# Later low parts, a later sample burst and later transpositions in the openings of two FFNs

## The chip, the cores and the metric

The kernel runs on one core of a Trainium2 chip. The metric is the device time of one launch in microseconds (us). The kernel before takes 2395.5 us, the median of three runs (2390.06 to 2398.54). One further execution was profiled; it took 2394.01 us, and its span from the first to the last instruction is 2392.4 us.

## The reference, cut to what matters

One decoder layer is computed for a prompt of 1024 tokens and a sample of 8 sequences of 4 new tokens, with D = 1024 and an FFN width of 2816:

```
x = x + 0.5 * gate0 * swiglu(modulated(x, g_ffn1, 0), w1_gate, w1_up, w1_down)
x = x + gate1 * mixers(modulated(x, g_mix, 1))          # attention beside gated MLP
x = x + 0.5 * gate2 * swiglu(modulated(x, g_ffn2, 2), w2_gate, w2_up, w2_down)
swiglu(h) = (silu(h @ w_gate) * (h @ w_up)) @ w_down
modulated(h) = rms_norm(h) * (1 + scale) + shift
```

The change lies in the first few dozen microseconds of the two swiglu lines.

## The kernel before, in words

**Engines and order.** Each engine works through its own queue in the order in which the program issues to it; the order is written out by hand. TensorE (PE) does the matmuls, ScalarE (ACT) copies and activations, VectorE (DVE) and GpSimd (POOL) the additions and subtractions, SyncE (SP) issues the loads. Nearly all tiles of the 1 MB-and-less kind share one pool of 46 buffers (`NU = 46`), and a load into a buffer waits for the last user of the tile that was there.

**Numbers in two parts.** A matrix is kept as a high part (rounded, made on ACT) and a low part (what is left, made on DVE as source minus high part). A product is three matmuls of 512 columns, high by high, high by low, low by high: `mm3`, L324 to L326. For token tiles the high part is `x_hi` (L742), the low part `x_lo` (L746); `x_put` does one right after the other. For weights of a block it is `split` (L330, L331).

**The FFN.** The 2816 hidden columns are done in 11 blocks of 256. Blocks 1 to 10 use a Strassen form with seven products, whose operands are tokens (B11, B21, B22), differences of tokens (T1 to T4) and sums of weights (`sums_s`, L256 to L259, four POOL additions `wsum`). Block 0 is done in the plain way, and meanwhile the differences are made: that is the opening. It has four stages (half, kh) = (0,0), (0,1), (1,0), (1,1), each of 48 matmuls: tokens 0 to 3 first, then 4 to 7, and the lower and upper half of D in turn. After each two `mm3` (six matmuls) `tick(1.36)` is called, so a stage has eight ticks, called turns 1 to 8 below.

**Fillers.** What is not block 0's own work is written as generators. A filler has a step cost (`every`) and a start value; each tick adds 1.36 to its account, and for each `every` in the account it is moved on to its next `yield`. `finish()` runs a generator to its end at once. `mid1` and `mid2` say which generators run in which stage of the first and second FFN:

- (0,0) of the first FFN: `second()` (L1822): the statistics of tokens 4 to 7 (Square on ACT L525, power on POOL L518 and L519, scaling on DVE L531), then `rows` for B12: for each of four j's four transpositions on PE (L553), their eviction on ACT (L756), `x_hi`, and the low part one j behind.
- (0,1): `rows` for B22, then `T1()`; beside it the sample's norm `s_norm`, which ends with two transpositions (L610) and the copy `xsT` on DVE (L612).
- (1,0): `T23()`, and `s_ffn_gu` for block 0 of the sample: a burst of 32 matmuls (L622) of the sample's rows against the unconverted weights of block 0, a copy `G` on DVE (L644), and two yields later the fold (`s_fold`: four transpositions L628, a reduction on DVE L630, a Silu on ACT L649, a product on DVE L651).
- (1,1): `T4()`, the loads of block 1's first weights and, at its middle, their `sums_s`.

In `T1`, `T23` and `T4` each step makes one difference (L776; T1 and T2 on DVE, T3 and T4 on POOL), then the high part on ACT and the low part on DVE:

```
sub_(nc.vector, t, f1[j][:, 1], f0[j][:, 0])                   # T2
sub_(nc.gpsimd, f1[j][:, 0], f1[j][:, 1], f1[j][:, 0])         # T3
self.x_put(X, "T2", j, t)
yield
```

`fin` (L863, L865) turns block 0's sums in PSUM into hidden rows: on ACT for the gate, on DVE for the up product. Block 1 begins with the product A11, whose weights are split into two parts just then; its third matmul needs the low part that DVE makes (L331).

Of the kernel before, what the change touches and what calls it, by code (L numbers as in the profile page):

```python
# [87 lines left out]
class Step:  # L88
# [682 lines left out]
    def x_rest(self, X, xs, sub, f0):  # L771


        nc = self.nc
        f1, t2 = [], []
        sub_ = lambda eng, o, x, y: eng.tensor_tensor(out=o, in0=x, in1=y, op=ALU.subtract)  # L776

        def rows(i, name):
            last = None
            for j in range(4):  # L780
                if not i:
                    f1.append(self.u([P, 2, 512], F32, name="xf"))
                self.x_tr(xs, sub, j, i, f1[j])
                w = self.x_hi(f1[j][:, i])
                if last:
                    self.x_lo(X, name, *last)
                last = (j, f1[j][:, i], w)
                yield
            self.x_lo(X, name, *last)
            yield  # L790

        def T1():
            for j in range(4):
                t = f0[j][:, 0]
                sub_(nc.vector, t, f1[j][:, 0], t)
                self.x_put(X, "T1", j, t)
                yield

        def T23():
            for j in range(4):  # L800
                if j % 2 == 0:
                    t2.append(self.u([P, 2, 512], F32, name="xt"))
                t = t2[j // 2][:, j % 2]
                sub_(nc.vector, t, f1[j][:, 1], f0[j][:, 0])
                sub_(nc.gpsimd, f1[j][:, 0], f1[j][:, 1], f1[j][:, 0])
                self.x_put(X, "T2", j, t)
                yield
                self.x_put(X, "T3", j, f1[j][:, 0])
                yield

        def T4():
            for j in range(4):
                t = f0[j][:, 1]
                sub_(nc.gpsimd, t, t, t2[j // 2][:, j % 2])
                self.x_put(X, "T4", j, t)
                yield

        return rows(0, "B12"), rows(1, "B22"), T1(), T23(), T4()

    def prod(self, un, X, ps, start=True, js=range(4), la=2):  # L820
# [940 lines left out]
def build(tc, a, o, stop=None):  # L1761
    with ExitStack() as ctx, tc.manual_schedule():
        k = Step(tc, a, o, ctx, stop)
# [8 lines left out]
        plan1 = k.plan_ffn("w1")  # L1772
        plan_m = k.plan_in()
        plan_p = [k.plan_post(hf == 1) for hf in range(2)]
        plan2 = k.plan_ffn("w2")
# [44 lines left out]
        f1a, f1b, T1, T23, T4 = k.x_rest(X1, xsb1, 0, f01)  # L1820

        def second():  # L1822

            for t in range(4, 8):
                xsb1.append(k.norm_stats(t, 0))
            for t in range(4, 8):
                k.norm_scale(t, 0, xsb1[t - 4])
            yield
            yield from f1a

        def chain(*gs):
            for g in gs:
                yield from g

        def mid1(stage):
            if stage == (0, 0):
                k.f1 = k.add(second(), 1.6)
            elif stage == (0, 1):
                k.f1.finish()
                for q in (2, 3):  # L1840
                    k.ada_q(q, k.psb)
                for q in (2, 3):
                    k.ada_m(q)
                for q in (2, 3):
                    k.x_mod(X1, f01, q)
                k.f1 = k.add(chain(f1b, T1), 1.1)
                k.f2 = k.add(k.s_norm(0, k.ada_rows()), 0.95)
            elif stage == (1, 0):
                k.f1.finish()
                k.f2.finish()  # L1850
                k.f1 = k.add(T23, 1.2)
                k.f2 = k.add(k.s_ffn_gu(plan1["b"][0]), 1.2)
            elif stage == (1, 1):
                k.f1.finish()
                k.f2.finish()
                k.f1 = k.add(T4, 1.3)
            elif stage == (2, 0):
                k.f1.finish()
            elif stage == 3:
                k.ad = k.add(k.ada_gen([2, 3, 4, 5], 4, 8), 2.6, 12.0)  # L1860
                k.ad.step()
# [8 lines left out]
        def after1(t):  # L1870
# [6 lines left out]
            if t == 3:  # L1877
                k.need(3, 4)
                k.norm_scale(3, 1, xs1[3])
                k.f1 = k.add(k.norm_T(xs1[0:4], 1, nT[0], k.psa), 4.0)  # L1880

        acc = k.ffn(plan1, X1, lambda: k.need(2) or k.gate[0], load_xp, mid1, after1)
        k.f1.finish()
        k.norm_scale(7, 1, xs1[7])
# [29 lines left out]
        f1 = k.add(k.c_T(cn1, 1), 1.3, 2.6)  # L1914
# [118 lines left out]
        def mid2(stage):  # L2033
            if stage == (0, 0):
                k.f1 = k.add(f1a2, 1.1, 5.5)
            elif stage == (0, 1):
                k.f1.finish()
                k.f1 = k.add(chain(f1b2, T1_2), 1.1)
                k.f2 = k.add(k.s_norm(2), 1.4)
            elif stage == (1, 0):  # L2040
                k.f1.finish()
                k.f2.finish()
                k.f1 = k.add(T23_2, 1.2)
                k.f2 = k.add(k.s_ffn_gu(plan2["b"][0]), 1.2)
            elif stage == (1, 1):
                k.f1.finish()
                k.f2.finish()
                k.f1 = k.add(T4_2, 1.3)
            elif stage == (2, 0):
                k.f1.finish()  # L2050
            elif stage == 3:
                k.load_gate(2)

# [21 lines left out]
        def last3(stage):  # L2075
# [9 lines left out]
            else:  # L2085
                fin(6, 0)
                nc.vector.scalar_tensor_tensor(out=r, in0=ss, scalar=1.0 / D, in1=r, op0=ALU.mult, op1=ALU.add)
                nc.gpsimd.tensor_tensor(out=r, in0=r, in1=k.mhalf[:, 0:1], op=ALU.pow)

        k.ffn(plan2, X2, lambda: k.gate[2], load_x2, mid2, after3, last3)  # L2090
        fin(7, 0, nc.scalar)
        fin(7, 1)
# [118 lines left out]
```

## Time and profile before

| what | value |
|---|---|
| median of three runs | 2395.5 us (2390.06 to 2398.54) |
| the profiled execution, its own time | 2394.01 us |
| its span | 2392.4 us |
| busy: PE, DVE, ACT, POOL | 96%, 57%, 34%, 36% |
| mean granted TensorE clock | 0.987 of 2.4 GHz |
| opening of the first FFN, first matmul of block 0 to first of block 1 | 30.23 to 109.20 us |
| opening of the second FFN, the same | 1687.23 to 1748.38 us |
| chain that ended last | PE 77%, issue 6%, DMA 5%, DVE 5%, ACT 3%, POOL 2% |

How to read it: busy is the time in which an engine had an instruction under way, as a share of the span. "Idle before" is the time for which an engine stood still ahead of an instruction, with the event that ended it. The granted clock is the clock that TensorE got: 1.00 is 2.4 GHz, 0.50 is 1.2 GHz. PE's matmuls overlap: one of 512 columns is recorded with 0.39 us at full clock, but the next starts 0.227 us after it.

### The profile page before, as it was taken

The page shows a single profiled execution, that of the slowest core. Times are in us where ns is not written, and L with a number is a line of the kernel's source. Part 1 is how long each engine was busy: PE and PEld are TensorE (multiplying, and loading weights), DVE is VectorE, ACT ScalarE, POOL GpSimd, SP SyncE. Part 2 cuts the span into 40 slices and gives each one's busy share as a digit, 9 for nine tenths or more (in the row PEclk, how much of TensorE's full clock was granted, in tenths as well). Part 3 has the DMA queues.
Part 4 walks back from the last instruction along what each step waited for, and adds up shares of the span by engine and source line. Part 5 has one row for each costly group of instructions (what it writes and reads, how often), then busy time and mean ns, then how long its engine had stood idle before and what let it go on. Part 6 is the DMA issues. An engine that isn't in the chain of part 4 may idle for free.

```text
span 2392.4 us, 37074 instructions
## 1 busy us (share of the span) xinstructions
PE 2294.7 (96%) x12989; PEld 1750.0 (73%) x12989; DVE 1372.9 (57%) x1897; ACT 819.4 (34%) x1411; POOL 858.0 (36%) x822
## 2 busy tenths in 40 slices
PE   6999999998998999999999999999899999999998
PEld 4678787876776775556677777777677878877876
DVE  3766666663556555674344455445666666666557
ACT  4322222323334244553332243222532223233433
POOL 1364556450125123243223310011156565552125
PEclk9899999999999999999999999999999999999999
DMA  6244444459855237568877725542144444358643
GB/s 264 84 144 139 158 137 150 154 182 383 328 184 184 110 80 220 173 183 227 226 212 217 234 77 194 186 139 83 63 151 151 144 150 152 135 184 305 239 155 142
DMA packets 192516, 420.10 MB, mean 176 GB/s; under 512 B 21981, under 2 KB 80298, under 8 KB 192330
## 3 DMA queue, kind: packets, MB, share of 16 engines
q1 hardware_dynamic: 179242, 381.01, 46.7%
q0 software_dynamic: 12800, 36.19, 5.4%
q8 instruction: 103, 1.69, 0.3%
q14 instruction: 83, 0.68, 0.1%
q10 hardware_dynamic: 288, 0.52, 0.1%
HBM read 337.31 MB, written 78.23 MB: 174 GB/s over the span
## 4 chain that ended last, share of the span: by engine, by line
PE 77%; issue 6%; DMA 5%; DVE 5%; ACT 3%; POOL 2%; POOLq 1%; SPq 1%; DVEq 0%; ACTq 0%
PE psa L324 15%; PE psa L325 15%; PE psa L326 15%; PE psb L324 7%; PE psb L325 7%; PE psb L326 6%; PE pss L622 3%; DVE wlo L187 1%; PE pss L1589 1%; POOLq L1546 1%; PE psa L1211 1%; PE psa L441 1%; DMA nat<-in_kvn 1%; DMA w<-in_w1d 1%; DMA wada<-in_w_ada 1%
## 5 line engine op out<-in xcount | busy, mean ns | idle before, releaser
L187 DVE TENSOR_TENSOR wlo<-w,whi 128x1024 fp32r<-128x1024 f32 (+1 forms) x273 | 304.3, 1153 | 163.5 <-ACT whi L186 138.0
L186 ACT CAST whi<-w 128x1024 fp32r<-128x1024 f32 (+1 forms) x273 | 243.5, 927 | 208.9 <-PE psb L325 61.1
L326 PE MATMUL psa<-xT,ws 128*128 128x512 f32 x800 | 311.7, 390 | 2.0 <-DVE ws L331 2.0
L324 PE MATMUL psa<-xT,ws 128*128 128x512 f32 x800 | 313.2, 391 | 0.0
L325 PE MATMUL psa<-xT,ws 128*128 128x512 f32 x800 | 311.2, 389 | 0.0
L331 DVE TENSOR_TENSOR ws<-wsum,ws 128x512 fp32r<-128x512 f32 x160 | 170.5, 1065 | 28.8 <-ACT ws L330 28.8
L869 POOL TENSOR_TENSOR h<-hf,h 128x512 f32<-128x512 f32 x60 | 97.6, 1627 | 235.7 <-issue 191.0
L326 PEld LDWEIGHTS psa<-xT,ws 128*128 128x128 f32 x800 | 150.1, 188 | 34.3 <-DVE ws L331 2.8
L325 PEld LDWEIGHTS psa<-xT,ws 128*128 128x128 f32 x800 | 150.3, 188 | 30.6
L324 PEld LDWEIGHTS psa<-xT,ws 128*128 128x128 f32 x800 | 150.2, 188 | 30.4
L324 PE MATMUL psa<-xT,whi 128*128 128x512 f32 x384 | 160.1, 417 | 1.6 <-ACT xT L742 1.6
L325 PE MATMUL psa<-xT,whi 128*128 128x512 f32 x384 | 153.0, 398 | 0.0
L326 PE MATMUL psa<-xT,wlo 128*128 128x512 f32 x384 | 152.5, 397 | 0.0
L325 PE MATMUL psa<-wlo,whi 128*128 128x512 f32 x308 | 122.3, 397 | 9.4 <-DVE wlo L187 9.4
L331 DVE TENSOR_TENSOR ws<-w,ws 128x512 fp32r<-128x512 f32 x120 | 111.4, 928 | 33.9 <-ACT ws L330 33.9
L324 PE MATMUL psa<-whi 128*128 128x512 f32 x308 | 123.0, 399 | 6.2 <-ACT whi L186 6.2
L324 PE MATMUL psb<-xT,ws 128*128 128x512 f32 x320 | 127.1, 397 | 0.0
L325 PE MATMUL psb<-xT,ws 128*128 128x512 f32 x320 | 125.1, 391 | 0.0
L326 PE MATMUL psb<-xT,ws 128*128 128x512 f32 x320 | 124.6, 389 | 0.0
L324 PE MATMUL psb<-whi 128*128 128x512 f32 x308 | 122.5, 398 | 0.0
L326 PE MATMUL psa<-whi,wlo 128*128 128x512 f32 x308 | 121.6, 395 | 0.0
L325 PE MATMUL psb<-wlo,whi 128*128 128x512 f32 x308 | 121.2, 393 | 0.0
(397 smaller groups left out, 4820.2 us busy)
## 6 DMA issues: line engine op xcount, KB each, us to landing
wada<-in_w_ada SPq DMA_DIRECT2D x72, 512.0 KB
x<-x SPq DMA_DIRECT2D x40, 512.0 KB
pk<-in_kvp SPq DMA_DIRECT2D x128, 144.0 KB
pk<-in_kvp POOLq DMA_DIRECT2D x128, 144.0 KB, 3.8
w<-w1h SPq DMA_DIRECT2D x35, 512.0 KB
w<-w2h SPq DMA_DIRECT2D x35, 512.0 KB
nat<-in_kvn SPq DMA_DIRECT2D x128, 128.0 KB
nat<-in_kvn POOLq DMA_DIRECT2D x128, 128.0 KB, 3.0
```

The costliest lines, as they stand in the source:

```text
L186: self.nc.scalar.copy(hv(w.hi), src)
L187: self.nc.vector.tensor_tensor(out=hv(w.lo), in0=src, in1=hv(w.hi), op=ALU.subtract)
L324: nc.tensor.matmul(out, sh, mh, start=first, stop=False, skip_group_check=cont)
L325: nc.tensor.matmul(out, sh, ml, start=False, stop=False, skip_group_check=cont)
L326: nc.tensor.matmul(out, sl, mh, start=False, stop=last, skip_group_check=cont)
L331: self.nc.vector.tensor_tensor(out=lo, in0=src, in1=hi, op=ALU.subtract)
L441: nc.tensor.matmul(ps[32 * k:32 * k + 32, 256 * qq:256 * qq + 256], self.sc[:, 4 * kh + k, :], t[:, k, :], start=(kh == 0), stop=(kh == 1))
L622: self.nc.tensor.matmul(ps[32 * j:32 * j + 32, cols], st[:, k, :], mv, start=(k < 4), stop=(k >= nk - 4))
L869: nc.gpsimd.tensor_tensor(out=g, in0=t, in1=g, op=ALU.mult)
L1211: nc.tensor.matmul(ps[:, c:c + n], q, K[:, c:c + n], start=True, stop=not diag)
L1546: v = eng.value_load(self.pt[0:1, 32 * b + i:32 * b + i + 1], min_val=0, max_val=self.a[name].shape[0] - 1)
L1589: nc.tensor.matmul(ps[32 * b:32 * b + 32, 0:256], self.sqT[:, ch, 4 * g + b, :], ts[b][:, :, ch, :], start=(ch == 0), stop=(ch == 2))
```

## The change

- `x_put` in T1, T23 and T4 becomes `put` and `low`: the high part is issued at once, the low part one step later (`low(1)` leaves one waiting), and the last low part when the generator ends (`low(0)`).
- The sample's burst for block 0 in both FFNs: the filler's step cost goes from 1.2 to 3.0, and it starts at minus 4.0. By the account above the burst moves from turn 1 to turn 6 of stage (1,0), and the fold from turn 3 of stage (1,0) to turn 2 of stage (1,1). The generator is finished at stage (2,0), no longer at (1,1).
- `second()` yields four times, not once, after the statistics, and its step cost goes from 1.6 to 1.15. The statistics are issued at turn 1 instead of 2; the transpositions of j = 0, 1, 2, 3 come at turns 5, 6, 6, 7 instead of 3, 4, 5, 6. Only the first FFN has this.

```diff
+        late = []
+        def put(name, j, src):
+            w = self.x_hi(src)
+            late.append((name, j, src, w))
+        def low(n):
+            while len(late) > n:
+                self.x_lo(X, *late.pop(0))
         def T1():
             for j in range(4):
                 t = f0[j][:, 0]
                 sub_(nc.vector, t, f1[j][:, 0], t)
-                self.x_put(X, "T1", j, t)
+                put("T1", j, t)
+                low(1)
                 yield
+            low(0)
...          (T23, once for T2 and once for T3, and T4 in the same way)
@@ second
-            yield
+            for _ in range(4):
+                yield
             yield from f1a
@@ mid1
             if stage == (0, 0):
-                k.f1 = k.add(second(), 1.6)
+                k.f1 = k.add(second(), 1.15)
@@ mid1 and mid2, the same edit in both
             elif stage == (1, 0):
-                k.f2 = k.add(k.s_ffn_gu(plan1["b"][0]), 1.2)
+                k.f2 = k.add(k.s_ffn_gu(plan1["b"][0]), 3.0, 4.0)
             elif stage == (1, 1):
                 k.f1.finish()
-                k.f2.finish()
             elif stage == (2, 0):
                 k.f1.finish()
+                k.f2.finish()
```

## Rows read from the trace of the kernel before

**Rows 1.** The page, part 1: busy time of each engine, its share of the span, and its instructions.
```profile
PE 2294.7 (96%) x12989; PEld 1750.0 (73%) x12989; DVE 1372.9 (57%) x1897; ACT 819.4 (34%) x1411; POOL 858.0 (36%) x822
```

**Rows 2.** Waits of PE over the whole span: who waited for whom, us in total, times, the longest.
```profile
PE psb L553 <- DVE xs L531: 19.6, 9, 10.9
...
PE pss L622 <- DVE xsT L612: 10.0, 2, 7.2
PE pss L488 <- DVE ms L466: 8.2, 1, 8.2
```

**Rows 3.** Timeline of PE, stage (0,0) of the first FFN: start and duration in us, the instruction, in brackets the idle time before it. The first and the last of the four transpositions of j = 0, and the first instruction after the stage's last matmul.
```profile
36.97 0.33 PE L553 MATMUL psb<-cst,xs 128*128 128x128 f32 x1
...
41.37 0.33 PE L553 MATMUL psb<-cst,xs 128*128 128x128 f32 x1 [1.14 <-DVE xs L531]
...
51.44 3.66 PE L362 MATMUL psb<-wada,sc 128*32 128x256 f32 x64
```

**Rows 4.** Stretches of the span: bounds in us and length; busy us (instructions) of PE, PEld, DVE, ACT, POOL; granted TensorE clock; DMA share; GB/s. In order: the wait of rows 3, what follows it, the burst of the second FFN, the loads for its block 1, and what follows two other waits of PE, of 2.93 and of 1.93 us.
```profile
36.90:41.50 4.60, 1.11 (x5) 0.54 (x5) 2.28 (x4) 1.44 (x4) 3.21 (x6) 1.00 0.95 377
41.50:45.00 3.50, 3.50 (x12) 2.81 (x13) 0.69 (x1) 1.40 (x2) 0.00 (x0) 0.52 0.08 29
1723.40:1727.80 4.40, 4.39 (x34) 2.11 (x35) 3.05 (x5) 1.14 (x2) 1.27 (x1) 0.50 0.00 0
1732.00:1736.00 4.00, 4.00 (x19) 3.27 (x19) 2.97 (x5) 1.48 (x3) 1.29 (x1) 1.00 0.73 266
535.90:539.00 3.10, 3.08 (x9) 2.40 (x9) 3.10 (x3) 0.00 (x0) 3.10 (x2) 0.61 0.98 328
2328.80:2331.50 2.70, 2.70 (x12) 2.23 (x13) 2.70 (x4) 2.25 (x3) 1.46 (x1) 1.00 0.97 246
```

**Rows 5.** Timeline of PE, later stages of the first FFN's opening: the sample's transpositions, the burst, the third matmul of block 1.
```profile
77.43 0.44 PE L610 MATMUL pss<-cst,u 128*128 128x128 f32 x2 [1.33 <-DVE u L603]
...
83.49 3.64 PE L622 MATMUL pss<-w,xsT 128*32 128x256 f32 x32 [2.85 <-DVE xsT L612]
...
110.81 0.50 PE L326 MATMUL psa<-xT,ws 128*128 128x512 f32 x1 [1.00 <-DVE ws L331]
```

**Rows 6.** Timeline of PE, the second FFN: the first matmul of stage (1,0), the burst, two matmuls that are 42 matmuls apart, the third matmul of block 1, and the same burst in block 1.
```profile
1714.60 0.47 PE L324 MATMUL psa<-xT,whi 128*128 128x512 f32 x1
...
1723.41 3.64 PE L622 MATMUL pss<-w,xsT 128*32 128x256 f32 x32 [7.17 <-DVE xsT L612]
...
1738.18 0.39 PE L324 MATMUL psa<-xT,whi 128*128 128x512 f32 x1
...
1747.70 0.39 PE L324 MATMUL psa<-xT,whi 128*128 128x512 f32 x1
...
1749.99 0.50 PE L326 MATMUL psa<-xT,ws 128*128 128x512 f32 x1 [1.00 <-DVE ws L331]
...
1763.41 1.93 PE L622 MATMUL pss<-w,xsT 128*32 128x256 f32 x32
```

**Rows 7.** Timeline of DVE, ACT and POOL, one whole step of T1 in the second FFN: the difference, the high part, POOL's own difference (of T3), the low part, the next difference.
```profile
1712.09 0.68 DVE L776 TENSOR_TENSOR xf<-xf 128x512 f32<-128x512 f32 x1
...
1712.81 0.62 ACT L742 CAST xT<-xf 128x512 fp32r<-128x512 f32 x1 [0.99 <-DVE xf L776]
...
1712.92 1.29 POOL L776 TENSOR_TENSOR xf<-xf 128x512 f32<-128x512 f32 x1 [4.90 <-DVE xf L776]
...
1713.46 1.29 DVE L746 TENSOR_TENSOR xT<-xf,xT 128x512 fp32r<-128x512 f32 x1 [0.69 <-ACT xT L742]
...
1714.68 0.68 DVE L776 TENSOR_TENSOR xf<-xf 128x512 f32<-128x512 f32 x1
```

**Rows 8.** Timeline of DVE, the second FFN: the last five low parts, the two up products of tokens 4 to 7, the first low part of block 1's weights.
```profile
1738.65 7.49 DVE L746 TENSOR_TENSOR xT<-xf,xT 128x512 fp32r<-128x512 f32 x5
1746.05 0.68 DVE L865 TENSOR_TENSOR h<-h,psa 128x512 f32<-128x512 f32 x1
1748.65 0.69 DVE L865 TENSOR_TENSOR h<-h,psa 128x512 f32<-128x512 f32 x1 [1.92 <-PE psa L326]
1749.26 0.68 DVE L331 TENSOR_TENSOR ws<-w,ws 128x512 fp32r<-128x512 f32 x1
```

**Rows 9.** Timeline of POOL in the same stretch: the first and the last of the four sums of block 1's weights.
```profile
1738.13 1.75 POOL L256 TENSOR_TENSOR wsum<-w 128x512 f32<-128x512 f32 x1
...
1743.24 1.74 POOL L259 TENSOR_TENSOR wsum<-w,wsum 128x512 f32<-128x512 f32 x1
```

**Rows 10.** Timeline of DVE and POOL in block 1: a DVE addition that reads PSUM, beside a POOL subtraction.
```profile
1755.36 0.69 DVE L885 TENSOR_TENSOR uv<-uv,psb 128x512 f32<-128x512 f32 x1 [0.57 <-PE psb L326]
...
1755.45 1.29 POOL L667 TENSOR_TENSOR wt<-wd 128x512 f32<-128x512 f32 x1 [1.82 <-issue]
```

**Rows 11.** Timeline of DVE, the first FFN: the first difference of T1, and the sample's two instructions that the transpositions of rows 5 wait for.
```profile
73.86 0.68 DVE L776 TENSOR_TENSOR xf<-xf 128x512 f32<-128x512 f32 x1
...
76.44 0.47 DVE L602 SCALAR_TENSOR_TENSOR u<-xsam,srs,ms 128x256 f32<-128x256 f32 x1
76.95 0.42 DVE L603 TENSOR_TENSOR u<-u,ms 128x256 f32<-128x256 f32 x1
```

**Rows 12.** Timeline of SP's queue: the two loads of block 1's first weights in the second FFN.
```profile
1731.08 1.26 SPq L163 DMA_DIRECT2D w<-in_w2g  x2
```

**Rows 13.** Timeline of SP's queue in the down product of the first FFN: eight loads, one behind the other.
```profile
570.30 8.69 SPq L1781 DMA_DIRECT2D x<-in_xp  x8
```

More of the change, by code (lines that the diff above doesn't have):

```diff
@@ L805, in T23 @@
                 sub_(nc.gpsimd, f1[j][:, 0], f1[j][:, 1], f1[j][:, 0])
-                self.x_put(X, "T2", j, t)
+                put("T2", j, t)
+                low(1)
                 yield
-                self.x_put(X, "T3", j, f1[j][:, 0])
+                put("T3", j, f1[j][:, 0])
+                low(1)
                 yield
+            low(0)
         def T4():
@@ L814, in T4 @@
                 sub_(nc.gpsimd, t, t, t2[j // 2][:, j % 2])
-                self.x_put(X, "T4", j, t)
+                put("T4", j, t)
+                low(1)
                 yield
+            low(0)
         return rows(0, "B12"), rows(1, "B22"), T1(), T23(), T4()
@@ L2043, in mid2 @@
                 k.f1 = k.add(T23_2, 1.2)
-                k.f2 = k.add(k.s_ffn_gu(plan2["b"][0]), 1.2)
+                k.f2 = k.add(k.s_ffn_gu(plan2["b"][0]), 3.0, 4.0)
             elif stage == (1, 1):
                 k.f1.finish()
-                k.f2.finish()
                 k.f1 = k.add(T4_2, 1.3)
@@ L2050, in mid2 @@
                 k.f1.finish()
+                k.f2.finish()
             elif stage == 3:
```

## The prediction

> **What bounds the kernel now.** I read the page first: PE is busy for 96% of the span [rows 1], so time is to be had only where PE stands still or runs slowly, and a microsecond saved there in an opening is one at the end, since the blocks behind it keep PE busy. Then the waits of PE [rows 2]: the two largest that the change can touch are the transpositions that wait for the scaling (19.6 us in all, 10.9 of them at the very start, which stays) and the sample's burst that waits for xsT (10.0, of which 7.2 in the second FFN). Then the timelines of PE. In stage (0,0) of the first FFN the transpositions of j = 0 start at 36.97 and the last of them waits until 41.37 for the last scaling [rows 3]. After this the granted clock is 0.52, that is mostly 1.2 GHz, for 3.5 us; after the burst's wait it is 0.50; a wait of 2.93 us is followed by 0.61, one of 1.93 us by 1.00 [rows 4]. The burst takes 3.64 us after its wait, 1.93 us in block 1 [rows 6].
>
> Last, why xsT is late: it stands in DVE's queue behind T1. One step of T1 there takes 2.59 us [rows 7]: difference, high part on ACT, low part. The low part is ready to go at 1713.46, but ends 0.54 us after POOL's subtraction (1712.92 + 1.29), and lasts 1.29 us instead of 0.68. So **DVE and POOL take turns** when both subtract in SBUF: five low parts beside four POOL sums need 8.0 us, 1738.13 to 1746.14, which is 5 x 0.60 + 4 x 1.29 = 8.2 [rows 8, 9]. An addition that reads PSUM runs beside POOL at its usual 0.69 [rows 10]. The wait for ACT that the change takes out of DVE's queue is thus largely POOL's turn already.
>
> **Part 1, the transpositions of the first FFN.** The scaling isn't sped up: turn 1 or turn 2, ACT, POOL and DVE have the same instructions ahead of it. On ACT the conversion of the next weights now precedes the evictions; ACT is idle there. PE does twelve more matmuls, 12 x 0.227 = 2.7 us (pace: 42 matmuls in 9.52 us [rows 6]), before it comes to the transpositions at 39.4, and still ends them at 41.4. Left to do are 18 matmuls and 12 transpositions, where 30 and 12 were left: 2.7 us sooner than 51.44. If the clock doesn't fall, another 1.8 us (half of 3.5). PE now stands nearly still for 1.6 us, not 4.5; of the waits of rows 4 that is nearer to 1.93, with no fall. I take 4.5, bounds 2.7 and 4.5. j = 1 and 2 come together and take the other two of three PSUM buffers; j = 3, six matmuls later, needs the eviction of j = 0, one ACT instruction, which is done by then. The next waits, for the adaLN products, keep their length.
>
> **Part 2, low parts later.** No instruction is added or dropped. xsT comes sooner, since T1's fourth low part goes behind it and DVE has no gap between steps. Low parts aren't needed before block 1; nothing waits for them but buffers.
>
> **Part 3, burst and fold later.** PE reaches the burst 36 matmuls later, 8.2 us into stage (1,0): 1722.8 in the second FFN. Before xsT DVE has 4 differences, 3 low parts and an up product, POOL 3 or 4 subtractions: from 1712.09 8 x 0.60 + 4 x 1.29 = 10.0 at most, so xsT is there by 1722.4, and the wait of 7.17 us goes, and with it the slow clock (1.7 us of the burst and some after it). What is late next? PE alone would run from 1714.60 [rows 6] 96 matmuls (21.8), the burst (1.93) and the fold (0.36) to 1738.7, and then 1.6 us to the third matmul of block 1, as now (block 1 begins at 1748.38): 1740.3. But that matmul waits for DVE, and DVE has all of T1 to T4 ahead of it: **the stall moves there.** From 1712.09: 8 differences, 16 low parts and the weights' low part, 25 x 0.60 = 15.0; POOL's 8 differences and 4 sums, 12 x 1.29 = 15.5; in turns, 30.5 us, to 1742.6. Below: POOL's sum lasts 1.75 where its turn is 1.29, so DVE holds it up by 0.46, not 0.60; twelve changes save 1.8 us: 1740.8. Above: seven DVE instructions on PSUM (copies, reduction, up products, 0.6 each) hide beside none of POOL's: 4.2 us more, 1746.8. I walked the three queues in program order with these durations: the changes and the PSUM instructions nearly cancel, 1742.7. The same walk through the order of before puts the weights' low part at 1749.25; the row says 1749.26 [rows 8]. So the third matmul comes at 1742.7 instead of 1749.99: **7.3 us**, bounds 3.2 and 9.2.
>
> The Trainium skill (SBUF — State Buffer, Who interferes with whom) says that a VectorE instruction with two SBUF inputs and a GpSimd one that reads SBUF exclude each other, and that the first holds the port for its whole instruction. By whole instructions of 0.68 the turns would sum to 32.5 us and the gain to 5.4; the rows show 0.46 to 0.60, and I keep those.
>
> The first FFN in the same way: from 73.86, with the sample's two instructions (0.8 [rows 11]) among them, 31.6 us by the walk, to 105.5 instead of 110.81 [rows 5]: **5.3 us**; the waits of 1.33 and 2.85 us go. Bounds: above 1.1, below 7.1 (PE alone: by the walk the sample's second instruction ends at 76.6, six matmuls later stage (1,0) begins, 78.0 + 24.1 + 1.6 = 103.7).
>
> PE now stands still for 2 to 3 us ahead of block 1's third matmul, where it was 1.0. That lies between the waits of 1.93 (no fall) and 2.93 (0.61 for some 3.1 us, 1.5 us lost [rows 4]). I take half, 0.75 at each, minus 1.5 together; bounds 0 and 3.0.
>
> The burst holds block 0's four raw tiles longer. Block 1's pair of loads is issued at 1731.08, once a low part has freed a buffer [rows 12], and lands by about 1736 (1.06 MB in rows 4). If it takes a raw tile's buffer it goes out behind the burst, 1724.8, and lands at 1730, ahead of POOL's turn at 1733: nothing. POOL's sums and ACT's copies for block 1 then move with it. DVE's copy G must come before the fold; the walk has it at 1730.4, PE at 1730.3: nothing.
>
> **Sum.** 4.5 + 5.3 + 7.3 - 1.5 = 15.6 us of 2394.0, the profiled execution's own time: 2378.4. The median of the runs is 1.5 higher; in its terms **2380**.
>
> **The rivals.**
> - *PE stays the bound.* If DVE and POOL cost less than I count, the gains are 4.5 + 7.1 + 9.7 = 21.3: 2374. For it: no PE wait but 1.0 us at block 1 today. Against: the turns of rows 8 and 9. Chance 0.12.
> - *The turns eat most of it.* PSUM instructions aren't hidden and the clock falls each time: 2.7 + 1.1 + 3.2 - 3.0 = 4.0, about 2391; halfway to my sum 2386. For it: DVE and POOL have no slack left in the opening. Against: the walk that met 1749.26. Chance 0.25, half of it short of a measurable gain.
> - *Slower: buffers.* The order in which 46 buffers come free changes for all that follows. Place: the down product of the first FFN, where loads queue one behind the other, 8 in 8.69 us [rows 13], and PE waits 8.2 us for one of them [rows 2]. If one load takes a buffer that only the next product frees, SP's whole queue stands behind it, up to one product, 132 matmuls x 0.227 = 30 us: 2410. It decides from 15.6 us of added wait. Against: the longest-free tile is taken as before. Chance 0.06.
> - *No effect* (the burst's wait only moves to block 1): against it is that DVE stands idle at 1746.73 for 1.92 us [rows 8], so today its queue isn't the bound. Chance 0.04.
>
> **How the numbers follow.** The forecast has 0.53. The range goes from 2372 (the first rival and some spread) to 2391 (the second); left out are the slower cases and the edges. 0.3%, 7.2 us, is about what a measurement of this kernel can tell from no change. Faster: 0.53 + 0.12 + 0.13 = 0.78; within: 0.12 + 0.03 (of the 0.04) = 0.15; slower: 0.06 + 0.01 = 0.07.
>
> **What would show it.** Right: in the waits, PE L622 on xsT gone in both FFNs, and the burst at 1.93 us; last transposition of j = 0 still at about 41.4 and the adaLN matmuls at about 47; PE's wait at L326 on DVE L331 of 2 to 3 us where it was 1.0, with DVE without a gap from T1 to there. Wrong: that wait over 5 us or under 1.5; the burst or the fold waiting; SP's pair of loads later than 1738 on the scale of before; new waits far from the openings, above all at 530 to 600 us.

## The result, and the profile after

The changed kernel takes **2381.89 us**, the median of six runs (2377.81 to 2386.02), beside 2394.49 us for six runs of the kernel before: a ratio of 0.9948, 95% interval 0.9934 to 0.9962. The forecast was 2380. In a second comparison (below) it took 2379.34 us; the twelve runs together have a median of 2380.8.

The profiled execution of after took 2386.02 us (span 2384.4), the slowest of its six. The page, part 1, in the columns of [rows 1]:

```profile
PE 2296.9 (96%) x12989; PEld 1752.9 (74%) x12989; DVE 1374.3 (58%) x1897; ACT 818.7 (34%) x1411; POOL 861.9 (36%) x822
```

The same instructions, the same busy time: what went is idle time and slow clock. PE's waits, in the columns of [rows 2]:

```profile
PE psb L553 <- DVE xs L531: 17.0, 8, 10.3
PE pss L488 <- DVE ms L466: 8.4, 1, 8.4
PE psa L326 <- DVE ws L331: 5.0, 2, 2.9
```

The burst's wait for xsT, 10.0 us before, isn't there any more; a new wait of 5.0 us stands at the third matmul of block 1. (Lines behind L790 have moved: L865 is now L882, L1589 is L1606.)

PE in stage (0,0) of the first FFN, the rows that answer to [rows 3]: the last transposition of j = 0, the matmul behind it, and the first instruction after the stage.

```profile
40.64 0.33 PE L553 MATMUL psb<-cst,xs 128*128 128x128 f32 x1 [1.14 <-DVE xs L531]
40.72 0.48 PE L324 MATMUL psa<-xT,whi 128*128 128x512 f32 x1
...
46.37 3.66 PE L362 MATMUL psb<-wada,sc 128*32 128x256 f32 x64
```

The scaling comes no sooner (its last transposition starts at 40.64, where it was 41.37 with a start-up 0.7 us longer), but from there to the end of the stage it takes 5.73 us, where it took 10.07.

The two openings further on, PE, for [rows 5] and [rows 6]: the sample's burst, the fold and block 1's third matmul, first FFN and second.

```profile
79.87 1.93 PE L622 MATMUL pss<-w,xsT 128*32 128x256 f32 x32
...
98.65 0.50 PE L326 MATMUL psa<-xT,ws 128*128 128x512 f32 x1 [2.09 <-DVE ws L331]
```
```profile
1717.72 1.93 PE L622 MATMUL pss<-w,xsT 128*32 128x256 f32 x32
...
1725.16 0.66 PE L628 MATMUL pss<-cst,G 128*128 128x128 f32 x4
...
1737.41 0.79 PE L326 MATMUL psa<-xT,ws 128*128 128x512 f32 x1 [2.94 <-DVE ws L331]
```

Burst and fold wait for nothing, and the burst lasts 1.93 us. DVE ahead of that last matmul, for [rows 8]: the four low parts of T4, the two up products, the low part of block 1's weights.

```profile
1730.86 4.70 DVE L746 TENSOR_TENSOR xT<-xf,xT 128x512 fp32r<-128x512 f32 x4
1735.48 1.27 DVE L882 TENSOR_TENSOR h<-h,psa 128x512 f32<-128x512 f32 x2
1736.68 0.68 DVE L331 TENSOR_TENSOR ws<-w,ws 128x512 fp32r<-128x512 f32 x1
```

There is no gap between them; the 1.92 us for which DVE waited for PE before the second up product are gone. DVE is the engine that PE now waits for. And SP's queue, for [rows 12]: the pair of loads goes out 12.2 us sooner than it did; 5.2 us of that the kernel was ahead already at 1690 us.

```profile
1718.85 4.31 SPq L163 DMA_DIRECT2D w<-in_w2g  x2
```

Last the stretches of [rows 4] (same columns): behind the transpositions, behind the wait of 2.09 us, and two in a row behind the wait of 2.94 us.

```profile
40.90:44.40 3.50, 3.50 (x21) 2.94 (x20) 1.61 (x3) 2.94 (x5) 0.00 (x0) 1.00 0.06 22
98.60:101.60 3.00, 2.95 (x13) 2.42 (x14) 2.93 (x5) 0.32 (x1) 1.12 (x1) 1.00 0.62 243
1737.40:1740.40 3.00, 2.99 (x7) 2.41 (x8) 2.93 (x5) 0.00 (x0) 1.16 (x1) 0.50 0.60 235
1740.40:1743.40 3.00, 3.00 (x8) 2.32 (x8) 1.37 (x2) 1.32 (x3) 0.63 (x1) 0.50 0.49 181
```

Behind the transpositions the granted clock is 1.00 (2.4 GHz) where it was 0.52. Behind the first new wait it stays at 1.00, behind the second it is 0.50 (1.2 GHz) for some 6 us: 7 and 8 matmuls in 3 us, not 13.

**Where the time came from.** Take the instructions of ACT and DVE that both kernels issue, subtract their start times, and take the median of a stretch: this says how much sooner the kernel is there than the first profile of before. What it rises by between two stretches was gained between them. The table does this for every profile of this study. The first three columns count from the stretch of 20 to 36 us: to 53 to 57 us (the transpositions), to 64 to 73 us (the last stretch ahead of T1), and to 125 to 300 us (all of the first FFN's opening). The fourth is the second FFN's opening (from 1690 to 1710 us to 1765 to 2000 us), and the last the stretch from 1130 to 1700 us, where no kernel is changed. All in us.

| profile | transpositions | up to T1 | first FFN | second FFN | 1130 to 1700 |
|---|---|---|---|---|---|
| after | 4.33 | 5.74 | 11.39 | 4.48 | -7.23 |
| after, again | 4.33 | 4.60 | 8.68 | 5.90 | -1.30 |
| before, again | 0.00 | 0.06 | 0.96 | -0.12 | -2.52 |
| low parts alone | 0.09 | 0.25 | 6.11 | 2.85 | -4.30 |
| burst alone | -0.02 | 1.36 | 2.17 | 4.11 | -3.03 |
| transpositions alone | 4.32 | 5.30 | 6.18 | -0.14 | -4.19 |
| without the burst's change | 4.32 | 5.41 | 11.27 | 2.84 | -6.04 |
| without the low parts' change | 4.33 | 5.33 | 5.95 | 2.51 | -1.98 |
| all differences on DVE | 4.31 | 5.38 | 12.48 | 6.59 | -0.20 |
| T4's low parts deferred | 4.33 | 5.60 | 12.37 | 9.35 | -3.59 |
| both of these | 4.32 | 5.33 | 12.66 | 9.40 | -3.34 |
| deferred, A11 earlier | 4.32 | 4.45 | 12.53 | 10.34 | -5.47 |

The change gains 15.9 us in its openings in one profile and 14.6 in the other; the forecast was 15.6.

What the second column adds to the first comes from the clock. Ahead of T1, PE waits 1.62 us for a high part of tokens in every profile, of before too, and behind that wait the granted clock stands at 0.50 for three to four us in some profiles and for six and more in others. The wait in before, then the stretch from 3 to 6 us behind it, in before, in after and in after, again:

```profile
59.14 0.79 PE L324 MATMUL psa<-xT,whi 128*128 128x512 f32 x1 [1.62 <-ACT xT L742]
...
62.14:65.14 3.00, 3.00 (x10) 2.50 (x9) 2.36 (x4) 2.66 (x5) 0.00 (x0) 0.50 0.00 0
57.07:60.07 3.00, 3.00 (x18) 2.59 (x17) 2.63 (x4) 2.97 (x6) 0.00 (x0) 0.94 0.01 3
57.14:60.14 3.00, 3.00 (x11) 2.54 (x10) 2.35 (x4) 2.66 (x5) 0.00 (x0) 0.54 0.01 3
```

This gives 1.0 to 1.4 us in eight of the twelve profiles, burst alone among them, which has no change up to there, and 0.1 to 0.3 us in the other four, one of them a profile of the changed kernel itself. So the change doesn't fix it; whether later transpositions make the short fall likelier (seven of nine profiles with them) isn't shown. Below, gains in the first FFN are therefore compared from T1 on: first FFN less up to T1.

### The profile page after: what moved, and what is told of

It reads as the page before. It is cut to its first block, busy times and chain, and to the rows that moved or that the text cites. A ratio compares the mean times of both kernels' runs of the same rounds, so it can differ in the third digit from the quotient of the medians.

```text
span 2384.4 us, 37063 instructions
## 1 busy us (share of the span) xinstructions
PE 2296.9 (96%) x12989; PEld 1752.9 (74%) x12989; DVE 1374.3 (58%) x1897; ACT 818.7 (34%) x1411; POOL 861.9 (36%) x822
## 4 chain that ended last, share of the span: by engine, by line
PE 77%; DVE 7%; DMA 5%; issue 4%; ACT 3%; POOL 2%; POOLq 1%; SPq 1%; DVEq 0%; ACTq 0%
PE psa L324 15%; PE psa L325 15%; PE psa L326 15%; PE psb L324 7%; PE psb L325 7%; PE psb L326 7%; PE pss L622 2%; DMA wada<-in_w_ada 2%; PE pss L1606 1%; DVE wlo L187 1%; DVE xT L746 1%; PE psa L1228 1%; DMA pk<-in_kvp 1%; PE psa L441 1%; DMA w<-in_w1d 1%
## 5 line engine op out<-in xcount | busy, mean ns | idle before, releaser
L326 PE MATMUL psb<-whi,wlo 128*128 128x512 f32 x308 | 121.8, 396 | 0.0
```

What stands on the lines that cost most here:

```text
L326: nc.tensor.matmul(out, sl, mh, start=False, stop=last, skip_group_check=cont)
```

## The experiments

**1. The changed kernel and the kernel before, once more.** No edit.

> The changed kernel once more, with a new profile. The first profile of it gained 11.4 us in the first FFN's opening and 4.5 us in the second's, but lost 4.5 us of that near 1150 us, 2.8 us from 1340 to 1550 us and 1.7 us near 2350 us, where the program is the same in both kernels. Theory: these are variations from run to run (waits for gathered rows, a clock that falls for some us), so the openings show the same gains to within 0.5 us, and the losses come at other places or with other sizes. Rival (the new order of buffers causes them): the same waits of 2.7 and 2.1 us come back at the same places, and the openings' 15.9 us can't be had whole. The time should be 2382 within 3 us in both cases.

> The kernel before, for a second profile of it. All eight profiles of changed kernels lost between 0.6 and 4.5 us against the first profile of before near 1160 us, at a wait for gathered rows and a clock below 1.00 there. Theory (variation: the first profile of before had a short wait there): this profile loses 1 to 4 us against the first at the same place, and the openings agree to within 1 us. Rival (the changed order of buffers makes them late there): the wait there is as short as in the first profile, 1.5 us, and nothing is lost.

The changed kernel took 2379.34 us (ratio to before 0.9935, interval 0.9920 to 0.9950), the kernel before 2394.24 (1.0001, 0.9990 to 1.0012). The large loss of the first profile of after did not come back (1.3 us against 7.2), though the wait near 1160 us was over 2 us again (2.73, then 2.32); and the second profile of before lost 2.5 us against the first in the same stretch, some of it at 1347 us, where a wait that was 0.85 us (and 2.09 us in the first profile of after) is now

```profile
1347.74 0.50 PE L324 MATMUL psb<-whi,mg 128*128 128x512 f32 x1 [2.13 <-ACT whi L186]
```

So "variation" holds for most of it, and what is said of the place near 1160 us fails: before waits 1.45 and 1.60 us there in its two profiles, and every changed kernel 1.6 us or more, up to 3.4. Whether about 1 us is given back there, by arriving sooner or by the changed order of buffers, stays open.

"To within 0.5 us" failed too: the first FFN's opening gained 11.39 and 8.68 us, and the clock did it (1.1 us ahead of T1, behind the wait of 1.62 us that both profiles have, and 1.6 us behind block 1's third matmul). The changed kernel again, behind the same two waits (2.10 and 2.94 us), two stretches each:

```profile
99.80:102.80 3.00, 2.91 (x9) 2.33 (x10) 2.93 (x6) 0.00 (x0) 1.08 (x1) 0.68 0.65 249
102.80:105.80 3.00, 3.00 (x12) 2.40 (x11) 1.94 (x2) 1.62 (x3) 0.70 (x1) 0.75 0.46 173
...
1732.60:1735.60 3.00, 2.93 (x7) 2.35 (x8) 2.93 (x6) 0.00 (x0) 1.09 (x1) 0.50 0.64 247
1735.60:1738.60 3.00, 3.00 (x14) 2.41 (x13) 1.93 (x2) 1.62 (x3) 0.69 (x1) 0.96 0.47 174
```

Behind 2.10 us the clock fell this time, behind 2.94 us it came back 3 us sooner. Before has the same: in its second profile the first FFN's burst, behind the same wait of 2.87 us, took 1.93 us at full clock, where [rows 5] has 3.64.

**2. One part alone, and all but one.** The edits are hunks of the change: (a) `put`/`low` in T1, T23 and T4 alone; (b) the filler's cost and its finish alone; (c) `second()` alone; (d) the change without (b); (e) the change without (a).

```diff
(a) -                self.x_put(X, "T1", j, t)
    +                put("T1", j, t)
    +                low(1)                       # T23, T4 alike
(b) -                k.f2 = k.add(k.s_ffn_gu(plan1["b"][0]), 1.2)
    +                k.f2 = k.add(k.s_ffn_gu(plan1["b"][0]), 3.0, 4.0)
...                  (finished at (2,0); the same in mid2)
(c) -                k.f1 = k.add(second(), 1.6)
    +                k.f1 = k.add(second(), 1.15)
...                  (and four yields ahead of f1a)
```

> Only the low parts one step behind are changed, against the kernel before; the sample's burst and the transpositions stay where they were. Theory (DVE and POOL take turns, so the wait for ACT is largely POOL's turn already): by the walk through the three queues the low part of block 1's weights in the second FFN ends 3.5 us sooner than in the kernel before, xsT 3.5 us sooner, so the burst's wait there falls from 7.2 to about 3.7 us, with the clock still falling behind it; in the first FFN 1 to 2 us. In all about 5 us, 2389.5. Rival 1 (the wait for ACT is a loss of its own, about 0.6 us at each of 16 steps): the burst's waits fall by all that PE can use, 8 us and more, 2386 or less. Rival 2 (the step order is hidden): no change, 2394.5, and the burst's waits stay at 7.2 and 2.9.

> Only the sample's burst and fold are later, in both FFNs, against the kernel before; every low part is made in its own step as before, and the transpositions stay. Theory: the burst's wait falls from 7.2 us to under 1.5 us in the second FFN and from 2.9 to none in the first, and the burst takes 1.93 us in the first; but DVE, which still waits in each step, is then late for block 1: by the walk its weights' low part ends 2.9 us sooner than before in the second FFN, so PE's wait ahead of block 1's third matmul grows from 1.0 to 6 us or more. In all 4 to 6 us, about 2389.5. Rival (PE stays the bound): that wait stays at 1 to 3 us and this part alone gives the whole 13 us of both FFNs, 2381.5. Rival (the wait only moves): no change, 2394.5, with a wait of over 8 us there.

> Only the transpositions of tokens 4 to 7 in the first FFN come later, against the kernel before. Theory: 2.7 us from twelve more matmuls ahead of the wait and 1.8 us from a clock that doesn't fall behind it, so 4.3 to 4.5 us from 51 us on, and the granted clock behind the last transposition of j = 0 is 1.00 where it was 0.52; 2390. Rival (the clock falls as before): 2.7 us, 2391.8. Rival (the gain is lost again at the waits for the adaLN products and at the burst of the first FFN): no change from 85 us on, 2394.5, with a burst's wait of over 6 us.

> The changed kernel with the sample's burst and fold back at their old turns; low parts and transpositions as changed. In the openings the low parts alone gave 6.1 us in the first FFN and 2.9 us in the second, the transpositions 4.3 to 5.0 us in the first, the later burst alone 2.2 and 4.1 us. Theory (the parts work on the same stall, so in the first FFN the low parts already give nearly all): 4.4 + 6.1 + 2.9 = 13.4 us from the openings where the whole change has 15.9, so 2.5 us slower than the changed kernel, 2384.5; the burst waits about 0.7 us in the first FFN and 3.8 us in the second, with the clock falling there alone. Rival (the parts add up): the later burst is worth 6.3 us, 2388 without it. Rival (the later burst only moves the wait): 2382 or less.

> The changed kernel with every low part made in its own step as before; transpositions and burst as changed. Theory (each part takes some of the same stall in the first FFN): transpositions 4.4 to 5.0 us there, the later burst 2.2 us and about 1 us that the earlier start of T1 gives; in the second FFN the later burst alone, 4.1 us; in all 11 to 12 us, 2384, with PE waiting 2 to 3 us at the fold for DVE's copy G. So the low parts are worth 2 to 5 us in the whole, and not the 9 us that they gave alone. Rival (the low parts carry the change): under 8 us, 2387.5 or more. Rival (they add nothing beside the later burst): 2380, as the changed kernel.

| kernel | us | ratio to before, 95% interval |
|---|---|---|
| (a) low parts alone | 2389.11 | 0.9967 (0.9953 to 0.9981) |
| (b) burst alone | 2391.44 | 0.9980 (0.9971 to 0.9990) |
| (c) transpositions alone | 2389.49 | 0.9972 (0.9961 to 0.9982) |
| (d) without the burst's change | 2381.92 | 0.9946 (0.9932 to 0.9959) |
| (e) without the low parts' change | 2385.60 | 0.9965 (0.9953 to 0.9977) |

(a) In the second FFN the burst's wait fell from 7.17 to 3.83 us, nearly as the walk had it (3.5 less), and the clock still fell. The first FFN gave 6.1 us where 1 to 2 were expected, 5.9 of them from T1 on: there the sample's transpositions wait 0.32 us and no longer 1.33, the burst 0.65 and no longer 2.85, and at that wait the clock stays up. PE's waits in this kernel:

```profile
PE pss L622 <- DVE xsT L612: 4.5, 2, 3.8
PE psa L326 <- DVE ws L331: 2.0, 2, 1.0
```

(b) The total was met (4.2 us by the medians where 4 to 6 were expected), the place was not. Nothing like 6 us at block 1 (1.3 and 1.0 us): the wait stood at the **fold**, which needs DVE's copy G, and G stood in the same slow queue. Of the 2.2 us in the first FFN 1.4 lie ahead of T1; from T1 on it gained 0.8 us, and before, again, 0.9 without any change. In (e), with the transpositions beside it:

```profile
PE pss L628 <- DVE G L644: 4.7, 2, 2.9
PE psa L326 <- DVE ws L331: 2.6, 2, 1.3
...
PE pss L622 <- DVE xsT L612: 0.5, 1, 0.5
```

(c) The transpositions gave 4.32 us, and 4.31 to 4.33 in all nine profiles that have them. None of it is lost again in the first FFN (6.18 us by 125 us, 1.0 of it from the clock ahead of T1); both rivals fall.

(d) and (e) settle the split. In the first FFN the low parts carry what follows the transpositions: from T1 on, 5.9 us with them and without the later burst (in (a) and in (d)), 0.6 with the burst and without them, 0.9 with neither. With both it is 5.7 and 4.1, so the later burst is worth nothing there. In the second FFN each helps: low parts alone 2.85, burst alone 4.1 or 2.5, both 4.5 or 5.9. The expectation for (e), 2 to 5 us for the low parts, was too low: 14.6 to 15.9 against 8.5 us in the openings. That of (d), 2.5 us for the burst, isn't settled: 2381.92 is 2.6 us above the changed kernel of the same comparison (2379.34), but within the intervals, and just at the rival's 2382, not at 2384.5. In the openings (d) has 14.1 us where the whole change has 15.9 and 14.6.

**3. The differences of T3 and T4 on DVE.** In T23 and T4 of the changed kernel:

```diff
-                sub_(nc.gpsimd, f1[j][:, 0], f1[j][:, 1], f1[j][:, 0])
+                sub_(nc.vector, f1[j][:, 0], f1[j][:, 1], f1[j][:, 0])
...
-                sub_(nc.gpsimd, t, t, t2[j // 2][:, j % 2])
+                sub_(nc.vector, t, t, t2[j // 2][:, j % 2])
```

> The changed kernel with all differences on DVE: those of T3 and T4 (8 in each FFN) move from POOL, where each took 1.29 us, to DVE, where each takes about 0.68. Theory (DVE and POOL take turns, so a subtraction moved off POOL saves the pair 1.29 minus 0.60 us): by the walk block 1's weights are ready 2.1 us sooner, PE's wait ahead of block 1's third matmul falls from 2.1 and 2.9 us to about 1 us in both FFNs, and the clock doesn't fall behind it; 3 to 5 us faster than the changed kernel, 2377 to 2379. Rival (the engines work side by side, and DVE alone is the bound): 8 more instructions of 0.68 us make DVE 5.4 us later in each opening, the wait grows to about 8 us, 2391 to 2394. Rival (PE is the bound there): no change, 2382, the waits as they are.

It took 2376.76 us (ratio 0.9922, 0.9908 to 0.9937). The interval reaches into that of the changed kernel's second comparison, so the rivals are judged by the waits: DVE isn't later by 5.4 us, and the waits didn't stay as they were. Both rivals that made DVE or PE the bound miss. The groups of DVE from T1's first difference to G, first in the changed kernel (18.2 us, 1706.86 to 1725.11), then here (14.0 us, 1701.10 to 1715.11); after the bar busy us and mean ns, then the idle time before them:

```profile
L746 DVE TENSOR_TENSOR xT<-xf,xT 128x512 fp32r<-128x512 f32 x7 | 5.9, 839 | 0.1
L746 DVE TENSOR_TENSOR xT<-xt,xT 128x512 fp32r<-128x512 f32 x3 | 4.4, 1469 | 0.9 <-ACT xT L742 0.7
L776 DVE TENSOR_TENSOR xf<-xf 128x512 f32<-128x512 f32 x4 | 4.3, 1085 | 0.0
```
```profile
L776 DVE TENSOR_TENSOR xf<-xf 128x512 f32<-128x512 f32 x8 | 5.4, 686 | 0.0
L746 DVE TENSOR_TENSOR xT<-xt,xT 128x512 fp32r<-128x512 f32 x4 | 2.8, 688 | 0.1
L776 DVE TENSOR_TENSOR xt<-xf 128x512 f32<-128x512 f32 x4 | 2.7, 685 | 0.0
```

DVE does three more subtractions up to G (the groups of the second fence run on to 1717.5, so they count a few more) and is there 4.2 us sooner: with POOL idle each lasts 0.69 us; beside POOL's subtractions the three groups have means of 0.84 to 1.47. That the two take turns is thus shown. But only part of it reaches block 1: from T1 to the third matmul 1.4 us in the first FFN and 0.7 in the second. In the second DVE now runs ahead of PE and waits 1.32 us for the fold, and T4's differences then stand beside POOL's sums. There the expected wait of 1 us with a full clock did not come either: PE waits twice, 2.05 us in all, and the clock is 0.50 in the 3 us behind.

```profile
1729.45 0.50 PE L324 MATMUL psa<-xT,ws 128*128 128x512 f32 x1 [1.26 <-ACT ws L330]
1730.97 0.79 PE L326 MATMUL psa<-xT,ws 128*128 128x512 f32 x1 [0.79 <-DVE ws L331]
```

**4. T4's last low parts behind block 1's first weights.** In the changed kernel, and in that of experiment 3:

```diff
         def T4():
...
-                low(1)
+                low(3)
                 yield
+            for _ in range(4):
+                yield
             low(0)
...
             elif stage == (2, 0):          # mid1 and mid2
-                k.f1.finish()
```

> The changed kernel, where the last three low parts of T4 are made behind the low parts of block 1's first weights and no longer ahead of them (T4 isn't needed before the sixth product of block 1). Theory (DVE's queue ahead of those weights is the stall of 2.1 and 2.9 us, and the clock falls behind the second): without three low parts the weights' low part comes 1 us behind the last matmul of block 0, as in the kernel before; the wait falls to 1.0 us in both FFNs, 1.1 and 1.9 us sooner, and the 2.9 us that the clock costs behind the longer wait are won back too: 5.9 us faster than the changed kernel, 2376. Rival (POOL's sums, or the high parts on ACT, are the limit): the wait stays over 2 us, 2381 to 2382. Rival (the three low parts come late for block 1, or hold buffers): new waits in block 1, 2384 or more.

> The kernel with all differences on DVE, where the last three low parts of T4 too are made behind the low parts of block 1's first weights. The kernel with all differences on DVE still waits 1.26 and 0.79 us ahead of block 1 in the second FFN, with a clock of 0.50 for 3 us behind it. Theory: the high parts of the weights come sooner on ACT and their low parts on DVE, PE waits 1.0 us there in all, and the clock stays up: 2.7 us faster than that kernel, 2374, and 20 to 22 us from the openings against the kernel before. Rival (PE is the bound there already, and the clock falls anyway): no change, 2376.8. Rival (DVE is late in block 1 with its 8 more instructions): new waits there, slower by 1 us or more.

They took 2375.81 us (0.9919, 0.9906 to 0.9933) and 2374.49 us (0.9914, 0.9899 to 0.9928); 2376 and 2374 were expected. The deferred kernel's third matmul of block 1 in both FFNs, and the stretch behind the second:

```profile
98.00 0.50 PE L326 MATMUL psa<-xT,ws 128*128 128x512 f32 x1 [1.00 <-DVE ws L331]
...
1732.60 0.50 PE L326 MATMUL psa<-xT,ws 128*128 128x512 f32 x1 [0.98 <-DVE ws L331]
```
```profile
1732.60:1735.60 3.00, 3.00 (x13) 2.50 (x14) 3.00 (x6) 0.40 (x1) 0.00 (x0) 1.00 0.59 229
```

Three subtractions of DVE in another order, and the wait is 1.0 us again and the clock stays at 1.00: DVE's queue was the stall. With the wait short, the differences' place no longer matters (9.35 and 9.40 us in the second FFN).

**5. The weights of A11 ahead of DVE's last up product.** In the deferred kernel, ahead of the last 12 matmuls of block 0:

```diff
                             for f in range(2):
...
+                                if half and kh and n == "u" and f:
+                                    self.conv_to(plan["b"][1]["g", "A11"] + 1, 0)
```

> The kernel with the last three low parts of T4 deferred, where in addition block 1's first weights (A11) are split into high and low part half a product earlier, ahead of DVE's last addition of block 0 and no longer behind it. Theory (the 1.0 us of PE that is left ahead of block 1's third matmul is DVE's queue, that addition and then the low part): the wait goes in both FFNs, 2.0 us faster than the kernel with the deferred low parts, 2373.8, which leaves no wait of PE for DVE in the openings but those at 40 to 62 us. Rival (the load of those weights or POOL's sums hold the high part up): the wait stays, or moves to the first matmul of block 1, 2375 to 2377. Rival (the tile taken earlier delays a load): slower.

It took 2373.04 us (0.9911, 0.9897 to 0.9925), and no wait for `ws` is left in either FFN. DVE there: the low part of the weights now stands between the two up products.

```profile
1730.85 0.68 DVE L884 TENSOR_TENSOR h<-h,psa 128x512 f32<-128x512 f32 x1
1731.98 0.69 DVE L331 TENSOR_TENSOR ws<-w,ws 128x512 fp32r<-128x512 f32 x1 [0.46 <-issue]
1732.60 0.68 DVE L884 TENSOR_TENSOR h<-h,psa 128x512 f32<-128x512 f32 x1
```

The second FFN gained 1.0 us more (10.34). The first did so too from T1 on (8.1 us against 6.8), though its whole opening doesn't show it (12.53 against 12.37): ahead of T1 this profile has 4.45 us and the deferred kernel's 5.60. The five runs of this kernel reach from 2369.8 to 2378.5, so it isn't shown that it is faster than the deferred one. All three versions of experiments 4 and 5 beat the kernel before; against the changed kernel their fifteen runs reach from 2369.8 to 2378.5 (medians 2373.0 to 2375.8), its twelve from 2374.1 to 2386.0 (median 2380.8).

## Why the prediction was right, step by step

**Part 1, transpositions: right.** 4.5 us forecast, 4.3 measured, in the change and alone, with the clock at 1.00 behind the wait as it was taken from the row of 1.93 us. That row was thin ground, and the clock's share (1.8 us) is in part luck: in the same trace the wait of 1.62 us at 59.14 us, as short as the one forecast, has a clock of 0.50 behind it (ahead of it PE does matmuls of one column, with waits between).

**Part 2, low parts: a sentence of it was wrong.** It says that DVE's wait for ACT is largely POOL's turn already; then the instructions would grow by about as much as the wait shrinks. Over the whole stretch from T1 to the weights' low part of the second FFN, the second profile of before (1714.62 to 1752.62, 38.0 us) and after (1706.86 to 1737.36, 30.5 us) have:

```profile
L746 DVE TENSOR_TENSOR xT<-xf,xT 128x512 fp32r<-128x512 f32 x13 | 15.3, 1202 | 3.0 <-ACT xT L742 3.0
L746 DVE TENSOR_TENSOR xT<-xt,xT 128x512 fp32r<-128x512 f32 x4 | 4.8, 1202 | 2.9 <-ACT xT L742 2.9
L776 DVE TENSOR_TENSOR xf<-xf 128x512 f32<-128x512 f32 x4 | 2.7, 679 | 0.0
```
```profile
L746 DVE TENSOR_TENSOR xT<-xf,xT 128x512 fp32r<-128x512 f32 x13 | 13.0, 1019 | 0.1
L746 DVE TENSOR_TENSOR xT<-xt,xT 128x512 fp32r<-128x512 f32 x4 | 6.0, 1488 | 1.1 <-ACT xT L742 0.8
L776 DVE TENSOR_TENSOR xf<-xf 128x512 f32<-128x512 f32 x4 | 4.3, 1085 | 0.0
```

The idle time ahead of the low parts falls from 5.9 to 1.2 us, and these instructions grow by 0.5 us only (22.8 to 23.3): nearly all of the wait was idle time. The turns exist (experiment 3), but they weren't hidden in that wait. The sum did not suffer, because the walk counted instruction by instruction and never used the sentence.

**Part 3, the burst and what follows: the walk right, in the first FFN for another part of the change.** The second FFN's third matmul of block 1 came 7.3 us sooner against the stretch ahead of the opening, 7.4 in the second profile, where 7.3 was forecast; T1 to the weights' low part took 30.5 us, as the walk had it, though not without a gap: 1.5 us of DVE's idle time are left, most of it waits for ACT. The plain sum of turns is 30.5 us too, but it leaves out this time and 4.7 us of instructions on PSUM, so its agreement proves little. By whole instructions, as the Trainium skill has it (SBUF — State Buffer, Who interferes with whom), it would be 32.5 by the prediction's estimate. The trace doesn't decide that rule: in experiment 3 DVE's subtractions with POOL idle last 0.69 us but start 0.60 us apart (eight from 1709.61 to 1713.82), so 0.60 can be the whole turn. In the first FFN 5.3 was forecast, and 7.1 and 5.9 were there ahead of the clock's fall at block 1. T1 began 1.4 and 0.3 us sooner than was counted on, against the end of stage (0,0) (67.39 in the first profile, where 73.86 less 5.07 was counted on), and this is the clock behind the wait of 1.62 us, which the prediction didn't count. From T1 to the third matmul both profiles took 31.3 us, where the walk had 31.6. What the prediction ascribed to the burst there belongs to the low parts (experiment 2): they were never walked alone.

**The clock: mis-sized.** 0.75 us was taken off at each new wait, half of the 1.5 us that the prediction read from the row of 2.93 us (the row gives 1.2 us, 0.39 of 3.1; the slow clock goes on to 540 us in that trace, 1.7 us in all). Between the third matmul and the stretch behind it the first profile lost 0.0 and 2.9 us, the second 1.6 and 1.5. That is 1.5 on average, twice the forecast, and about the upper bound of 3.0 for the two together in each profile.

**The sum.** 4.5 + 5.3 + 7.3 - 1.5 = 15.6 us; the openings gave 15.9 (4.3 + 7.1 + 7.3 - 2.9, to rounding) and 14.6 (4.3 + 5.9 + 7.4 - 3.1). That the first is so near is luck: what the clock cost more at block 1 came back as the 1.4 us ahead of T1. Of these, 12.6 and 16.0 us are found in the two comparisons of the medians, 2394.49 to 2381.89 and 2395.35 to 2379.34. The rivals: PE did not stay the bound (the new waits), though it became so once three low parts were moved, and then gave 9.35 us in the second FFN, where the prediction had 9.7 for it. Of a buffer that holds up the first FFN's down product nothing is seen: PE's wait there is 8.4 us where it was 8.2, and the pair of loads went out long before 1738.

## What to carry to other kernels

When work is moved off one wait, walk the queue of the engine behind it to the next thing that needs it: here the stall went from the burst to block 1's weights, at the size that the walk gave, and the next step (three subtractions that nobody needs yet, ahead of one that PE waits for) could have been read from the same walk. Before a gain is put down to one part of a change, walk each part alone; two parts that empty the same queue don't add up. What a slow clock costs behind a wait differs between two profiles of one kernel by more than a microsecond, so take a second profile before explaining a place by it.

## What the hardware showed that was not expected

- The granted clock behind a wait isn't set by the wait's length alone. Behind 2.09 us it was 1.00 and behind 2.10 us 0.68, in two profiles of one kernel; behind 2.94 us it was 0.50 for 6 us and for 3 us (the fences above, both at block 1's third matmul). Behind a single wait of 1.0 us ahead of that matmul it fell in no profile (13 such waits in eight profiles, with 1.00 in the 3 us behind each).
- It also fell where PE counts as busy nearly throughout, at a place that the change doesn't touch: in the first profile of after behind sixteen matmuls of one column each (1.84 us) and a wait of 0.26 us. In the first profile of before it stayed up behind the same instructions (four transpositions in 0.66 us and not 0.93). First after with the stretch behind, then before:

```profile
1533.04 1.84 PE L476 MATMUL pss<-cst,gm 128*128 128x1 f32 x16
1535.14 0.93 PE L628 MATMUL pss<-cst,G 128*128 128x128 f32 x4 [0.26 <-DVE mod L483]
...
1535.10:1538.50 3.40, 3.36 (x11) 2.79 (x12) 1.02 (x2) 1.67 (x4) 0.00 (x0) 0.54 0.95 277
...
1542.00 0.66 PE L628 MATMUL pss<-cst,G 128*128 128x128 f32 x4 [0.26 <-DVE mod L483]
```

- Eight subtractions moved from POOL to DVE, 5.5 us of DVE's time, made DVE's stretch up to the weights' low part 0.7 us shorter (29.8 against 30.5 us).
